# Second modulation, first half: weighted rows added up on VectorE and summed over partitions once, in place of matmuls per block

## The chip, the cores and the metric

One core of one Trainium2 chip. The metric is device microseconds for one execution of the whole program. The engines are called by their short names: PE (TensorE), DVE (VectorE), ACT (ScalarE), POOL (GpSimd), SP (SyncE, which issues the large loads).

## The reference, cut to what matters

The program is two transformer blocks one after the other. The change lies in the first one. A vector `c` of 1024 elements gives six rows of 1024 (shift, scale and gate, twice), which modulate the sequence (256 tokens, 1024 features) ahead of the token mixer and ahead of the mixture of experts:

```
sc = silu(c)
shift1, scale1, gate1, shift2, scale2, gate2 = split(sc @ w_mod + b_mod, 6)   # w_mod: 1024 x 6144
h = modulate(rms_norm(x, norm1_g), shift1, scale1)      # h * (1 + scale) + shift
y, yc = token_mixer(h, hc, P, last)                      # attention, GLA and Hyena branches
x = x + gate1 * y
h = modulate(rms_norm(x, norm2_g), shift2, scale2)
x = x + gate2 * grouped_moe(h, router_w, ...)            # 16 experts
```

"The second modulation" is the product for the last 4096 columns (gate1, shift2, scale2, gate2): `sc` (1024 long) times a 1024 x 4096 matrix, plus the bias `b_mod2`. Half 0 is its first 2048 columns. The token mixer projects `h` into columns for three branches, works them, weighs each by a gate, and merges:

```
m = sigmoid(g_hy) * (y_hy @ w_br_hy) + sigmoid(g_gla) * (y_gla @ w_br_gla) + sigmoid(g_att) * (y_att @ w_br_att)
y = m @ w_out
```

All data are float32. Most products are made as three F32R matmuls of high and low parts (`mm3`).

## The kernel before, in words

**Loads and splits.** SP loads weights as `raw` tiles of 128x2048 (1 MB) in an order that is fixed ahead (`take`, L552, gives them out; `load` issues the next ones when slots are free). Each matrix that goes through `mm3` is split into `w`: a high part by ACT and a low part by DVE, in pieces of 128x1024. The matrices of the second modulation are not split.

**The stage.** The loop over branches (L1414 on, inside `program`) runs attention, GLA, Hyena. In each it takes four blocks of gate columns (`w_brg`: 48 h matmuls of 128x256 each, rows `ps<-hH,w` and `ps<-hL,w`), in the attention branch six blocks of Hyena columns (`hyena_cols`, whose evacuations are the `uc` rows on ACT and DVE: one ACT activation, then two DVE operations on it, twice a block), in the GLA branch the `gate_cols`, and then the branch product (`w_br_att`: rows `ps<-ya,w`; `w_br_gla`: rows `ps<-yg,w`).

**Side jobs.** Attention, GLA and Hyena are generators beside these columns. `Side.tick` (L383 on) runs the next step of a job after a group of matmuls, when a model clock on PE, ACT and DVE (`Clocked`, L341) says that its inputs are there; so the order of the program is set when it is built, from the costs of the operations issued so far. An attention step for head h is `turn(h-2)` (transposes `ps<-c_base,e`, copied by ACT to `pT`), `scores(h)`, `weigh(h-3)` (rows `ps<-pT,kv`, split into `ya`), softmax and normalization.

**Second modulation.** Sixteen blocks of 128x2048, `mod_block(i)` (L1353), are put between the columns: blocks 0 to 3 behind the four `w_brg` blocks of attention, 4 to 7 behind the four `w_br_att` blocks, 8 to 15 in the other branches. For each, `mod_rows` (L815) issues four float32 matmuls (128x32 `cs` as the stationary operand, 512 columns each, the trace has two records for each) that go to four groups of 32 partitions of one PSUM bank, and over eight blocks add up to one half of the modulation. At the eighth the bias (`bm`) is added on DVE, and the generator `mod_spread` splits the 128x512 into `mrow`, spreads each 512 columns over all partitions by K=32 matmuls with `pick`, and copies them into `mod2` tiles. For half 0 it goes on: one of its tiles is transposed (`turned_half`, rows `ps<-c_base,mod`, copied to `h2T`), router logits are made of it (`ps<-par,h2T`), and DVE copies them to `shifted`. Each of blocks 8 to 15 first runs one step of that generator.

**End of the GLA branch.** DVE normalizes the GLA output into `oy`; PE transposes it (`ps<-c_base,oy`), ACT and DVE split that into `yg`, and `ps<-yg,w` follows. The Hyena job then transposes `uc` into `z`, multiplies by the transform (`z,fwd`) and goes on through `Y` (parts `YH`, `YL`).

Of the kernel before, what the change touches and what calls it, by code (L numbers as in the profile page):

```python
# [10 lines left out]
F32R = mybir.dt.float32r  # L11
I32 = mybir.dt.int32
AF = mybir.ActivationFunctionType
OP = mybir.AluOpType
# [4 lines left out]
D = 1024  # L19
# [363 lines left out]
class Side:  # L383
# [10 lines left out]
    def next(self):  # L394

        a = self.jobs[:2]
        return a[1] if len(a) > 1 and a[1][2] is a[0][0] and a[1][1] < a[0][1] else a[0]
# [22 lines left out]
def program(ctx, tc, A, out, dump=None):  # L420
# [5 lines left out]
    V, S, G, P = nc.vector, nc.scalar, nc.gpsimd, nc.tensor  # L426
    V, S, P = Clocked(V, "V"), Clocked(S, "S"), Clocked(P, "P")
# [4 lines left out]
    def T(shape, name, dt=F32, tag=None):  # L432
        n = 4
        for s in shape[1:]:
            n *= s
        if tag is None:
            for t, lim in (("us", 128), ("uh", 512), ("u1", 1024), ("u2", 2048), ("u4", 4096), ("u8", 8192)):
                if n <= lim:
                    tag = t
                    break  # L440
        uid[0] += 1
        t = sb.tile(list(shape), dt, tag=tag, bufs=BUFS.get(tag, 1), name=f"{name}{uid[0]}")
        return t

    def T2(shape, name):

        n = 4 * math.prod(shape[1:])
        if n > 4096:
            return T(shape, name + "H", F32R), T(shape, name + "L", F32R)
        t = T([shape[0], 2, *shape[1:]], name, F32R)  # L450
        return t[:, 0], t[:, 1]

    def PS(name="ps"):
        uid[0] += 1
        t = pp.tile([128, 512], F32, tag="ps", bufs=8, name=f"{name}{uid[0]}")
        return t
# [6 lines left out]
    def split(h, l, src):  # L463
        S.activation(h, src, AF.Copy)
        V.tensor_tensor(l, src, h, op=OP.subtract)
# [86 lines left out]
    def take(name, b, u=0):  # L552
        i, v = pieces[pos["take"]]
        assert order[i][:2] == (name, b) and u == v, (order[i], v, name, b, u)
        stream()
        pos["take"] += 1
        return halves.pop((i, u)) if order[i][4] is not None else raws.pop(i)
# [66 lines left out]
    def feat_block(name, b, x, per=1):  # L624

        for u in range(2):
            wh, wl = take(name, b, u)
            for j in range(per):
                g = u * per + j
                if g % 2 == 0:  # L630
                    ps = PS()
                lin_feat(wh, wl, j, x, ps[:, (g % 2) * 256:(g % 2) * 256 + 256])
                side.tick()
                if g % 2:
                    yield ps
# [10 lines left out]
    def C(name):  # L646
        g, sl = CCOLS[name]
        return cg[g][:, sl]
# [35 lines left out]
    pick = T([128, 128], "pick", F32R)  # L684
# [7 lines left out]
    st = {}  # L692
# [119 lines left out]
    cs = T([128, 8, 32], "cs", tag="cs")  # L812
    V.memset(cs, 0.0)

    def mod_rows(w, k, ps):  # L815
        for j in range(4):
            P.matmul(ps[32 * j:32 * j + 32], cs[:, k], w[:, 0, j * 512:j * 512 + 512], start=k == 0, stop=k == 7)
# [46 lines left out]
    mrow = T([128, 512], "mrow")  # L864
# [41 lines left out]
    def by_k(pair):  # L906
        return lambda k: (pair[0][:, k], pair[1][:, k])
# [164 lines left out]
    ps = PS()  # L1072
# [276 lines left out]


    acc2, mod2, spreads = {}, [], []

    def mod_block(i):  # L1353

        hf, k = divmod(i, 8)
        w = take("mod2", i)
        if hf:
            next(spreads[0], None)
        if k == 0:
            acc2[hf] = PS("mod")  # L1360
        mod_rows(w, k, acc2[hf])
        if k == 4:
            st["bm"] = bm = T([128, 512], "bm", tag="u4")
            V.memset(bm, 0.0)
            for j in range(4):
                S.dma_start(bm[32 * j:32 * j + 1], A["b_mod2"][:, hf * 2048 + j * 512:hf * 2048 + j * 512 + 512])
        if k == 7:
            bm = st["bm"]
            V.tensor_tensor(bm, acc2.pop(hf), bm, op=OP.add)
            spreads.append(mod_spread(st.pop("bm")))  # L1370
            if False:
                next(spreads[hf])

    rw = Pc("router_w").rearrange("p (k e) -> p k e", k=8)

    def turned_half(src, k4):
        pt = PS()
        for k in range(4):
            P.transpose(pt[:, k * 128:k * 128 + 128], src[:, (4 * k4 + k) * 128:(4 * k4 + k) * 128 + 128], ident)
        t = T([128, 512], "h2T")  # L1380
        S.activation(t, pt, AF.Copy)
        return t

    def logits(ts, ps, start, stop):

        for k in range(8):
            P.matmul(ps, ts[k // 4][:, k % 4 * 128:k % 4 * 128 + 128], rw[:, k], start=start and k == 0, stop=stop and k == 7)

    def mod_spread(rows):

        rH, rL = T2([128, 512], "mrow")
        split(rH, rL, rows)
        yield
        for a in range(2):
            t = T([128, D], "mod2")
            for n in range(2):
                ps = PS()
                q = slice(32 * (2 * a + n), 32 * (2 * a + n) + 32)
                P.matmul(ps, pick[q], rH[q], start=True, stop=False)
                P.matmul(ps, pick[q], rL[q], start=False, stop=True)  # L1400
                S.activation(t[:, n * 512:n * 512 + 512], ps, AF.Copy)
            mod2.append(t)
        yield
        if len(mod2) == 2:
            ts = [turned_half(mod2[1], k4) for k4 in range(2)]
            yield
            ps = PS()
            logits(ts, ps[:, :16], True, True)
            st["shifted"] = T([128, 16], "shifted", tag="uh")
            V.tensor_copy(st["shifted"], ps[:, :16])  # L1410

    msum = mH = mL = None
    n_mod = 0
    for b, br in ((2, "att"), (1, "gla"), (0, "hy")):  # L1414
        g = T([128, 8, 256], "gate")
        for j in range(4):
            ps, = feat_block("w_brg", 4 * b + j, by_k(hs[0]))
# [18 lines left out]
        for i in range(8 // per):  # L1436
            for j, ps in enumerate(feat_block("w_br_" + br, i, ys, per // 2)):
                c = slice(per * i + 2 * j, per * i + 2 * j + 2)
# [156 lines left out]
    def ahead(v, count):  # L1595
# [21 lines left out]
                           op0=OP.is_lt, op1=OP.mult)  # L1617
    low(0, 1)

    ps = PS()  # L1620
# [75 lines left out]
    with tc.If(full > CAP, label="full"):  # L1696
# [11 lines left out]
        for e in range(N_EXP):  # L1708
            def fetch(k, i, q):
                t = fw[turn[0] % 2]  # L1710
                turn[0] += 1
                b, c = i // 2, i % 2 * 2 + q
                if k == "down" and b % 2 and e > N_EXP - 3:
                    b, c = 2 * (N_EXP - 2 + q) + 1, e % 2 * 2 + i % 2
                nc.sync.dma_start(t, A["moe_" + k][b, :, c * 512:c * 512 + 512])
                return t

            for k in range(8):
                for q in range(2):
                    w = fetch("gu", 8 * e + k, q)  # L1720
                    for m in range(2):
                        P.matmul(gu[q, m], fT[m][:, k * 128:k * 128 + 128], w, start=k == 0, stop=k == 7)
            for m in range(2):
                hf, ht, ps = hfs[m], hts[m], gu[0, m]
# [6 lines left out]
            for k in range(4):  # L1731
                for n in range(2):
                    w = fetch("down", 4 * e + k, n)
# [89 lines left out]
    for w, n in (("a", 8), ("b", 16)):  # L1823
# [4 lines left out]
        k = T([128, 2 * n], "rk", tag="us")  # L1828
# [26 lines left out]
    for e in range(N_EXP):  # L1855
# [3 lines left out]
        ps = PS()  # L1859
# [504 lines left out]
```

## Time and profile before

| | |
|---|---|
| median of 3 runs | 1422.9 us (1419.89 to 1423.99) |
| profiled execution | 1417.77 us, span 1416.0 us |
| mean granted PE clock | 0.994 |
| PE busy | 1365.2 us, 96% of the span |
| DVE busy | 836.7 us, 59% |
| ACT busy | 635.8 us, 45% |

The span goes from the first to the last instruction of the profiled execution; its own time lies 1.8 us over the span. Nearly all operations are issued through one wrapper and carry its line, L379; so one reads the trace by the names of tiles. A row such as `mod<-raw,cs` gives the tile written and those read. Matmuls are pipelined and the ends in their rows are modelled, so for PE the distance from start to start is read, not the length of one record. Durations and stalls all come from this one execution.

### The profile page before, as it was taken

What the parts mean: (1) busy time and instruction counts of PE and PEld (TensorE: products, weight loads), DVE (VectorE), ACT (ScalarE), POOL (GpSimd) and SP (SyncE); (2) the same over time, 40 slices, a digit from 0 to 9 for tenths busy, and PEclk for the clock granted to TensorE, in tenths of its full rate; (3) what the DMA queues carried; (4) which work ended last, traced back from release to release, by engine and by line L of the source; (5) the groups of instructions that cost most, each with busy time, mean ns of one, the idle gap of its engine ahead of it and who ended that gap; (6) DMA issues with size and microseconds to landing.
All of it is one profiled execution on the core that took longest, in us unless ns stands there. A gap on an engine that the chain in (4) does not pass through costs nothing.

```text
span 1416.0 us, 20480 instructions
## 1 busy us (share of the span) xinstructions
PE 1365.2 (96%) x8334; PEld 1064.8 (75%) x8334; DVE 836.7 (59%) x1517; ACT 635.8 (45%) x1021; POOL 8.3 (1%) x15
## 2 busy tenths in 40 slices
PE   5999999999999899999999899999999998999998
PEld 2678899878797444343488679999978887999996
DVE  4777457445866511211475586666676888566675
ACT  4643465534433311111356555445536664455541
POOL 0000000000000000000000000000000000000000
PEclk9999999999999999999999999999999999999999
DMA  9523334635469799999742345655544354555630
GB/s 370 223 71 119 149 150 153 250 125 190 175 212 360 301 421 421 421 421 421 283 179 90 120 149 181 207 179 208 175 156 146 127 179 139 188 179 180 216 140 30
DMA packets 44482, 297.42 MB, mean 210 GB/s; under 512 B 5171, under 2 KB 6371, under 8 KB 10017
## 3 DMA queue, kind: packets, MB, share of 16 engines
q1 hardware_dynamic: 41868, 291.02, 54.6%
q10 hardware_dynamic: 1924, 3.27, 0.7%
q0 software_dynamic: 592, 1.79, 0.5%
q8 instruction: 67, 1.10, 0.3%
q14 instruction: 31, 0.25, 0.0%
HBM read 295.00 MB, written 1.05 MB: 209 GB/s over the span
## 4 chain that ended last, share of the span: by engine, by line
PE 58%; DVE 5%; ACT 2%; issue 1%; DVEq 0%; ACTq 0%
PE ps L379 48%; PE pd L379 7%; DVE w L379 1%; PE pa L379 1%; PE pq L379 1%; ACT pe L379 1%; DVE v L379 1%; PE oc L379 1%; DVE sm L379 1%; DVE rs L379 0%; ACT w L379 0%; DVE xL L379 0%; DVE rsa L379 0%; ACT xH L379 0%; ACT oc L379 0%
## 5 line engine op out<-in xcount | busy, mean ns | idle before, releaser
L379 DVE TENSOR_TENSOR w<-raw,w 128x1024 fp32r<-128x1024 f32 (+3 forms) x301 | 346.5, 1195 | 84.6 <-ACT w L379 83.5
L379 ACT ACTIVATE w<-raw 128x1024 fp32r<-128x1024 f32 (+3 forms) x301 | 293.5, 1033 | 10.8 <-DVE w L379 4.8
L379 PE MATMUL ps<-xH,w 128*128 128x256 f32 x1408 | 256.5, 283 | 0.6 <-ACT xH L379 0.6
L379 PEld LDWEIGHTS ps<-xH,w 128*128 128x128 f32 x1408 | 220.6, 192 | 1.8 <-ACT xH L379 1.1
L379 PE MATMUL ps<-xL,w 128*128 128x256 f32 x704 | 199.4, 283 | 0.7 <-DVE xL L379 0.7
L379 PE MATMUL ps<-w,xH 128*128 128x512 f32 (+2 forms) x544 | 150.3, 362 | 4.0 <-ACT xH L379 2.1
L379 PEld LDWEIGHTS ps<-xL,w 128*128 128x128 f32 x704 | 135.0, 192 | 1.8 <-DVE xL L379 1.1
L379 PE MATMUL pd<-w,fh 128*128 128x512 f32 x528 | 125.6, 395 | 0.0
L379 PE MATMUL ps<-raw,xg 128*64 128x512 f32 x512 | 120.0, 600 | 0.0
L379 PE MATMUL ps<-hH,w 128*128 128x256 f32 (+1 forms) x608 | 115.7, 287 | 0.0
L379 PEld LDWEIGHTS pd<-w,fh 128*128 128x128 f32 x528 | 98.2, 189 | 21.6
L379 PEld LDWEIGHTS ps<-w,xH 128*128 128x128 f32 x544 | 95.4, 189 | 19.3 <-ACT xH L379 4.0
L379 PEld LDWEIGHTS ps<-hH,w 128*128 128x128 f32 (+1 forms) x608 | 94.9, 187 | 7.9 <-issue 2.7
L379 PE MATMUL ps<-w,xL 128*128 128x512 f32 (+2 forms) x272 | 97.8, 360 | 1.9 <-DVE xL L379 1.7
L379 PE MATMUL ps<-w,hH 128*128 128x512 f32 (+1 forms) x288 | 88.1, 390 | 0.0
L379 PE MATMUL ps<-hL,w 128*128 128x256 f32 (+1 forms) x304 | 85.9, 283 | 0.0
L379 PEld LDWEIGHTS ps<-raw,xg 128*64 128x64 f32 x512 | 33.3, 137 | 55.7 <-issue 51.9
L379 DVE SCALAR_TENSOR_TENSOR fc<-ps,par,fc 128x255 f32<-128x255 f32 x88 | 42.4, 482 | 51.5 <-ACT fc L379 49.9
L379 ACT ACTIVATE fc<-ps,par 128x256 f32<-128x256 f32 x44 | 24.8, 564 | 92.3 <-PE ps L379 66.4
L379 PEld LDWEIGHTS ps<-w,hH 128*128 128x128 f32 x288 | 52.2, 188 | 13.8 <-issue 2.7
L379 PEld LDWEIGHTS ps<-w,xL 128*128 128x128 f32 x272 | 51.3, 189 | 11.9 <-DVE xL L379 5.1
L379 PE MATMUL ps<-raw,hid 128*64 128x512 f32 x256 | 57.4, 593 | 0.0
(445 smaller groups left out, 1858.7 us busy)
## 6 DMA issues: line engine op xcount, KB each, us to landing
raw<-in_moe_gu SPq DMA_DIRECT2D x63, 1024.0 KB, 14.1
raw<-in_moe_down SPq DMA_DIRECT2D x32, 1024.0 KB, 12.8
raw<-in_mod SPq DMA_DIRECT2D x24, 1024.0 KB, 5.0
raw<-in_ffn_gate SPq DMA_DIRECT2D x22, 1024.0 KB, 4.8
raw<-in_ffn_up SPq DMA_DIRECT2D x22, 1024.0 KB, 4.9
raw<-in_ffn_down SPq DMA_DIRECT2D x22, 1024.0 KB, 4.8
raw<-in_w_brg SPq DMA_DIRECT2D x12, 1024.0 KB, 5.9
raw<-in_ple_gate SPq DMA_DIRECT2D x8, 1024.0 KB, 4.8
```

The costliest lines, as they stand in the source:

```text
L379: return f(*args, **kw)
```

## The change

In half 0 (blocks 0 to 7) PE's matmuls go. A tile `acc` of 128x2048 is cleared on DVE at block 0, and its row 0 is loaded with the bias by a DMA on ACT's queue. In each of the eight blocks DVE adds the matrix, row by row times the block's column of `cs`, into `acc`, in two operations of 128x1024. At block 7 the new generator `mod_sums` takes the place of `mod_spread` for this half: for each 1024 columns it splits `acc` into `mrow` parts (ACT and DVE), and four F32R matmuls with a 128x128 matrix of ones sum over the partitions and spread the sum over all of them at once; ACT copies the results to `mod2`. Then come the transposes and the logits as before. The generator has five steps where `mod_spread` had four for this half, and blocks 8 to 15 still run one each. Half 1 stays as it was.

```diff
--- before.py
+++ after.py
@@ -1349,13 +1349,27 @@
 
 
     acc2, mod2, spreads = {}, [], []
+    ones = T([128, 128], "pick", F32R)
+    S.activation(ones, C("ones16"), AF.Copy, scale=16.0)
 
     def mod_block(i):
 
         hf, k = divmod(i, 8)
         w = take("mod2", i)
-        if hf:
-            next(spreads[0], None)
+        if not hf:
+
+            if k == 0:
+                st["acc"] = acc = T([128, 2048], "acc")
+                V.memset(acc, 0.0)
+                S.dma_start(acc[0:1], A["b_mod2"][:, :2048])
+            acc = st["acc"]
+            for n in range(2):
+                c = slice(n * 1024, n * 1024 + 1024)
+                V.scalar_tensor_tensor(acc[:, c], w[:, 0, c], cs[:, k, 0:1], acc[:, c], op0=OP.mult, op1=OP.add)
+            if k == 7:
+                spreads.append(mod_sums(st.pop("acc")))
+            return
+        next(spreads[0], None)
         if k == 0:
             acc2[hf] = PS("mod")
         mod_rows(w, k, acc2[hf])
@@ -1368,8 +1382,6 @@
             bm = st["bm"]
             V.tensor_tensor(bm, acc2.pop(hf), bm, op=OP.add)
             spreads.append(mod_spread(st.pop("bm")))
-            if False:
-                next(spreads[hf])
 
     rw = Pc("router_w").rearrange("p (k e) -> p k e", k=8)
 
@@ -1385,6 +1397,27 @@
 
         for k in range(8):
             P.matmul(ps, ts[k // 4][:, k % 4 * 128:k % 4 * 128 + 128], rw[:, k], start=start and k == 0, stop=stop and k == 7)
+
+    def mod_sums(acc):
+
+        for a in range(2):
+            rH, rL = T2([128, D], "mrow")
+            split(rH, rL, acc[:, a * D:a * D + D])
+            yield
+            t = T([128, D], "mod2")
+            for n in range(2):
+                ps = PS()
+                for r in (rH, rL):
+                    P.matmul(ps, ones, r[:, n * 512:n * 512 + 512], start=r is rH, stop=r is rL)
+                S.activation(t[:, n * 512:n * 512 + 512], ps, AF.Copy)
+            mod2.append(t)
+            yield
+        ts = [turned_half(mod2[1], k4) for k4 in range(2)]
+        yield
+        ps = PS()
+        logits(ts, ps[:, :16], True, True)
+        st["shifted"] = T([128, 16], "shifted", tag="uh")
+        V.tensor_copy(st["shifted"], ps[:, :16])
 
     def mod_spread(rows):
 
@@ -1401,14 +1434,6 @@
                 S.activation(t[:, n * 512:n * 512 + 512], ps, AF.Copy)
             mod2.append(t)
         yield
-        if len(mod2) == 2:
-            ts = [turned_half(mod2[1], k4) for k4 in range(2)]
-            yield
-            ps = PS()
-            logits(ts, ps[:, :16], True, True)
-            st["shifted"] = T([128, 16], "shifted", tag="uh")
-            V.tensor_copy(st["shifted"], ps[:, :16])
-
     msum = mH = mL = None
     n_mod = 0
     for b, br in ((2, "att"), (1, "gla"), (0, "hy")):
```

DVE, block 0 of the modulation in the attention branch, behind the low part of a gate column's weights. Before:

```order
228 L379 TENSOR_TENSOR w_1354<-raw_1262,w_1354 128x1024
229 L379 TENSOR_TENSOR ya_1417<-ps_1412,ya_1417 128x256
230 L379 TENSOR_REDUCE nb_1420<-ps_1404 128x1
231 L379 TENSOR_SCALAR nb_1420<-nb_1420,rs_640 128x1
232 L379 TENSOR_REDUCE nb_1423<-ps_1408 128x1
233 L379 TENSOR_SCALAR nb_1423<-nb_1423,rs_719 128x1
```

Now (`acc` is the new sum, `raw` the modulation matrix, `cs` the weights of its rows):

```order
228 L379 TENSOR_TENSOR w_1356<-raw_1264,w_1356 128x1024
229 L379 MEMSET acc_1361 128x2048
230 L379 SCALAR_TENSOR_TENSOR acc_1361<-raw_990,cs_105,acc_1361 128x1024 x2
231 L379 TENSOR_TENSOR w_1393<-raw_1366,w_1393 128x1024
232 L379 TENSOR_TENSOR ya_1446<-ps_1441,ya_1446 128x256
233 L379 TENSOR_REDUCE nb_1449<-ps_1433 128x1
234 L379 TENSOR_SCALAR nb_1449<-nb_1449,rs_640 128x1
```

The memset and the two additions of block 0 stand ahead of `ya` and the softmax rows behind it; so does the next low part `w`, which stood behind those rows before.

PE, the last attention steps, ahead of the branch product `ya,w` (`c_base,e`: the transposes of `turn`; `pT,kv`: `weigh`; `hH,w` and `hL,w`: Hyena columns). Before, first `turn(7)` and `weigh(6)`, and 34 rows later `weigh(7)`:

```order
697 L379 MATMUL ps_2063<-hH_315,w_1938 128x256
698 L379 MATMUL ps_2118<-c_base_80,e_1894 128x128 x4
699 L379 MATMUL ps_2124<-c_base_80,e_1897 128x128 x4
700 L379 MATMUL ps_2130<-pT_2001,kv_592 128x256 x4
701 L379 MATMUL ps_2147<-hH_315,w_1973 128x256
702 L379 MATMUL ps_2147<-hL_316,w_1973 128x256
```

```order
733 L379 MATMUL ps_2147<-hL_316,w_2025 128x256
734 L379 MATMUL ps_2147<-hH_315,w_2025 128x256
735 L379 MATMUL ps_2207<-pT_2117,kv_592 128x256 x4
736 L379 MATMUL ps_2214<-ya_1417,w_2060 128x256 x6
737 L379 MATMUL ps_2214<-ya_1634,w_2060 128x256 x6
```

Now:

```order
726 L379 MATMUL ps_2098<-hL_316,w_1952 128x256
727 L379 MATMUL ps_2098<-hH_315,w_1952 128x256
728 L379 MATMUL ps_2183<-c_base_80,e_2016 128x128 x4
729 L379 MATMUL ps_2189<-c_base_80,e_2019 128x128 x4
730 L379 MATMUL ps_2195<-pT_2123,kv_592 128x256 x4
731 L379 MATMUL ps_2203<-pT_2182,kv_592 128x256 x4
732 L379 MATMUL ps_2210<-ya_1446,w_2032 128x256 x6
```

`turn(7)`, `weigh(6)` and `weigh(7)` follow one another behind the last Hyena column, with the branch product right behind.

PE, end of the GLA branch (`oy`: transposes of the normalized output; `mrow,pick` in the second listing: the matmuls with ones for the second 1024 columns). Before:

```order
1037 L379 MATMUL ps_3088<-hH_315,w_2962 128x256
1038 L379 MATMUL ps_3140<-c_base_80,oy_3012 128x128 x2
1039 L379 MATMUL ps_3140<-c_base_80,oy_3032 128x128 x2
1040 L379 MATMUL ps_3147<-c_base_80,oy_3012 128x128 x2
1041 L379 MATMUL ps_3147<-c_base_80,oy_3032 128x128 x2
1042 L379 MATMUL ps_3160<-par_63,h2T_3073 128x16 x4
1043 L379 MATMUL ps_3160<-par_63,h2T_3080 128x16 x4
1044 L379 MATMUL mod_2657<-raw_2931,cs_105 32x512 x4
1045 L379 MATMUL ps_3182<-yg_2994,w_3035 128x256 x24
```

Now:

```order
1025 L379 MATMUL ps_3049<-hH_315,w_2934 128x256
1026 L379 MATMUL ps_3101<-c_base_80,oy_2984 128x128 x2
1027 L379 MATMUL ps_3101<-c_base_80,oy_3004 128x128 x2
1028 L379 MATMUL ps_3108<-c_base_80,oy_2984 128x128 x2
1029 L379 MATMUL ps_3108<-c_base_80,oy_3004 128x128 x2
1030 L379 MATMUL ps_3122<-mrow_3040,pick_1258 128x512 x2
1031 L379 MATMUL ps_3126<-mrow_3040,pick_1258 128x512 x2
1032 L379 MATMUL mod_2584<-raw_2837,cs_105 32x512 x4
1033 L379 MATMUL ps_3141<-yg_2966,w_3007 128x256 x24
1034 L379 MATMUL ps_3171<-yg_2966,w_3035 128x256 x24
1035 L379 MATMUL ps_3203<-c_base_80,mod_3121 128x128 x4
1036 L379 MATMUL ps_3210<-c_base_80,mod_3121 128x128 x4
```

The matmuls with ones stand where the router logits (`par,h2T`) stood; the transposes of `mod`, before 34 rows ahead of `oy`, come two product groups behind it, and the logits have left the listing for a place after the first Hyena transform.

DVE at the same place. Before:

```order
388 L379 TENSOR_TENSOR oy_3032<-o_2584,rs_3020 128x512
389 L379 TENSOR_TENSOR oy_3032<-oy_3032,gog_2844 128x512
390 L379 TENSOR_TENSOR w_3035<-raw_2965,w_3035 128x1024
391 L379 TENSOR_TENSOR w_3063<-raw_2965,w_3063 128x1024
392 L379 TENSOR_TENSOR w_3113<-raw_3086,w_3113 128x1024
393 L379 TENSOR_TENSOR yg_2994<-ps_3140,yg_2994 128x512
394 L379 TENSOR_TENSOR yg_2994<-ps_3147,yg_2994 128x512
```

Now:

```order
395 L379 TENSOR_TENSOR oy_3004<-o_2660,rs_2992 128x512
396 L379 TENSOR_TENSOR oy_3004<-oy_3004,gog_2716 128x512
397 L379 TENSOR_TENSOR w_3007<-raw_2937,w_3007 128x1024
398 L379 TENSOR_TENSOR w_3035<-raw_2937,w_3035 128x1024
399 L379 TENSOR_TENSOR mrow_3040<-acc_1361,mrow_3040 128x1024
400 L379 TENSOR_TENSOR w_3074<-raw_3047,w_3074 128x1024
401 L379 TENSOR_TENSOR yg_2966<-ps_3101,yg_2966 128x512
402 L379 TENSOR_TENSOR yg_2966<-ps_3108,yg_2966 128x512
```

A split of `acc` into `mrow` has come between the second and the third low part `w`, ahead of the evacuations `yg`.

## Rows read from the trace of the kernel before

**Rows 1.** Page, part 1: busy time, share of the span and instructions of each engine.
```profile
PE 1365.2 (96%) x8334; PEld 1064.8 (75%) x8334; DVE 836.7 (59%) x1517; ACT 635.8 (45%) x1021; POOL 8.3 (1%) x15
```

**Rows 2.** Windows, 170 to 290 us: stretch and length, busy us (instructions) per engine, clock, DMA.
```profile
170.00:180.00 10.00, 10.00 (x73) 8.60 (x72) 5.58 (x11) 4.93 (x9) 0.00 (x0) 1.00 0.44 178
...
sum 120.00, PE 120.00 PEld 106.64 DVE 68.88 ACT 69.77 POOL 0.00; mean PE 10.00 PEld 8.89 DVE 5.74 ACT 5.81 POOL 0.00
```

**Rows 3.** Groups by form on PE, 160 to 290 us: count, busy us, mean ns, idle.
```profile
L379 PE MATMUL mod<-raw,cs 128*32 128x512 f32 x64 | 8.5, 605 | 0.0
```

**Rows 4.** Tile `mod`: count, duration ns min/median/max, first and last start, form.
```profile
L379 PE MATMUL mod<-raw,cs x192: 592/593/1062, 13.8 to 400.3; 128*32 128x512 f32 x192
...
L379 DVE SCALAR_TENSOR_TENSOR mod<-mod,g2n x1: 1225/1225/1225, 446.1 to 446.1; 128x1024 f32<-128x1024 f32 x1
```

**Rows 5.** Timeline of PE around one block: start, us, engine, operation, count [idle before].
```profile
186.58 1.07 PE L379 MATMUL mod<-raw,cs 128*32 128x512 f32 x8
187.58 0.39 PE L379 MATMUL ps<-hH,w 128*128 128x256 f32 x1
```

**Rows 6.** Timeline of DVE, a memset in the GLA branch.
```profile
282.84 0.91 DVE L379 MEMSET att<- 128x1024 f32 x1 [0.16 <-issue]
```

**Rows 7.** Timeline of DVE, start of two attention steps.
```profile
173.31 0.42 DVE L379 TENSOR_TENSOR ya<-ps,ya 128x256 fp32r<-128x256 f32 x1 [5.64 <-ACT ya L379]
...
184.24 0.42 DVE L379 TENSOR_TENSOR ya<-ps,ya 128x256 fp32r<-128x256 f32 x1 [4.21 <-ACT ya L379]
```

**Rows 8.** Page, part 6: DMA issues, KB each, median us to landing.
```profile
raw<-in_mod SPq DMA_DIRECT2D x24, 1024.0 KB, 5.0
```

**Rows 9.** Timeline of SP's queue, the load of block 2.
```profile
158.67 0.33 SPq L515 DMA_DIRECT2D raw<-in_mod  x1
```

**Rows 10.** Timeline of PE, spreading half 0 and the block behind it.
```profile
314.21 0.74 PE L379 MATMUL ps<-mrow,pick 32*128 32x512 f32 x6
...
315.96 1.07 PE L379 MATMUL mod<-raw,cs 128*32 128x512 f32 x8
```

**Rows 11.** Timeline of PE, 128x512 F32R matmuls of the `gate` columns.
```profile
329.84 0.63 PE L379 MATMUL ps<-w,hH 128*128 128x512 f32 x2
...
330.53 0.62 PE L379 MATMUL ps<-w,hH 128*128 128x512 f32 x2
```

**Rows 12.** Timeline of ACT, end of the hyena columns.
```profile
238.60 1.08 ACT L379 ACTIVATE pT<-ps 128x512 f32<-128x512 f32 x2 [1.43 <-PE ps L379]
...
246.51 0.56 ACT L379 ACTIVATE uc<-ps,par 128x256 f32<-128x256 f32 x1 [1.38 <-PE ps L379]
248.15 0.56 ACT L379 ACTIVATE uc<-ps,par 128x256 f32<-128x256 f32 x1 [1.07 <-DVE uc L379]
```

**Rows 13.** Timeline of PE, end of attention.
```profile
237.96 1.04 PE L379 MATMUL ps<-c_base,e 128*128 128x128 f32 x8
...
246.31 1.89 PE L379 MATMUL ps<-pT,kv 128*128 128x256 f32 x8
247.85 1.43 PE L379 MATMUL ps<-ya,w 128*128 128x256 f32 x9
```

**Rows 14.** Timeline of DVE, end of the GLA branch.
```profile
349.86 3.49 DVE L379 TENSOR_TENSOR w<-raw,w 128x1024 fp32r<-128x1024 f32 x3
353.26 1.28 DVE L379 TENSOR_TENSOR yg<-ps,yg 128x512 fp32r<-128x512 f32 x2
```

**Rows 15.** Timeline of PE, end of the GLA branch.
```profile
341.72 1.04 PE L379 MATMUL ps<-c_base,mod 128*128 128x128 f32 x8
...
350.70 1.86 PE L379 MATMUL ps<-par,h2T 128*128 128x16 f32 x16
```

**Rows 16.** Waits of PE, 330 to 420 us: total us, times, longest.
```profile
PE ps L379 <- ACT z L379: 1.1, 1, 1.1
PE ps L379 <- DVE z L379: 1.1, 1, 1.1
PE ps L379 <- DVE YL L379: 0.8, 1, 0.8
```

## The prediction

> **What bounds the kernel now.** I read the page's busy line first: PE is busy 96% of the span, DVE 59%, ACT 45% [rows 1]. That is an average, so next I read busy time by stretch, where the change works: from 170 to 290 us PE is busy 120.00 us of 120, DVE 68.88, which leaves DVE 51 us idle [rows 2]. There no engine but PE sets the pace: a PE microsecond taken out should shorten the program, a DVE microsecond put in costs nothing while nobody waits for it. The granted clock is 1.00 there, the 2.4 GHz level, so no change of clock enters the sum.
>
> **What is removed.** 64 records of `mod<-raw,cs` stand between 160 and 290 us; together they cover 8.5 us of PE [rows 3]. One record takes 593 ns [rows 4], but the eight of a block run side by side: they start at 186.58, and the next h matmul starts at 187.58 [rows 5], 1.00 us a block and 8.0 for eight by that distance, 8.5 by the grouped row. I take the grouped row, as it holds all eight blocks: **-8.5 us**. Summing single records would give 64 x 0.593 = 38 us; the window shows that they overlap. In the Trainium skill, "TensorE: Matmul & The Clock Gate", section "Measured speedup vs the span model", three column tiles are given 2.38 times the speed of matmuls one behind the other. By that figure alone a block would be an estimated 8 x 0.593 / 2.38 = 2.0 us and the saving 16; the trace shows 1.00 to 1.07, so the measurement decides.
>
> **What is added on DVE.** Sixteen 128x1024 operations of two tensors and a scalar. The trace has that kind once, 1225 ns [rows 4]: 19.6 us. A memset of 128x1024 takes 0.91 [rows 6], so about 1.8 for 128x2048. Two 128x1024 `mrow` splits come in place of one of 128x512, and the `bm` add goes. That is some 23 us into 51 us of idle. The idle lies in pieces: DVE idles 5.64 us before the attention step at 173.31 and 4.21 before the one at 184.24 [rows 7]. A block's 2.45 us fits in either. The tight place is block 0: memset 1.8, then the `b_mod2` row by a DMA on ACT's queue, on which the accumulations wait, then 2.45. The DMA is between nothing and the 5.0 us that a whole megabyte of `in_mod` takes [rows 8]; even at 5.0 the sum, 9.3 us, overruns 5.64 by 3.6, and the next gap of 4.21 absorbs it. Priced at 0. Behind a waiting accumulation stand the low parts of `w` and `ya`, which PE needs; if that cover is gone each block costs up to its 2.45 (rival B). ACT's second `w` split of the block stands behind the DMA issue, with the same reserve.
>
> `acc` also holds one slot of the size that SP's loads use, from block 0 to the second split, so an SP load can have to wait for one more release. Block 2's matrix is issued at 158.67 [rows 9] and read at 186.58 [rows 5], 28 us ahead with 5.0 to land. Priced at 0. The order on SP and POOL does not change.
>
> **Spreading the sums.** Before, eight K=32 matmuls spread half 0: from 314.21 to the next block at 315.96, 1.75 us [rows 10]. After, eight 128x512 F32R matmuls by `ones`; three of that size take 0.69 us (329.84 to 330.53) [rows 11], so 8 x 0.23 = 1.8, entered at two places rather than one: **+0.3**, ends 0 and 0.5.
>
> **The end of attention.** The side jobs are placed by a model clock, in which PE has become cheaper and DVE dearer, so they come later in PE's row. `weigh(7)` stood 34 rows behind `turn(7)`; now `turn(7)`, `weigh(6)` and `weigh(7)` follow one another. `weigh(7)` needs both copies of `pT`, which stand on ACT behind two `uc` activations with DVE's `uc` work between: from the first `uc` at 246.51 to the end of the second, 248.71, then the two copies, 1.08: 3.28 us [rows 12], and the first starts 0.20 after PE's group is through (246.31, where `weigh` follows it). PE has `turn(7)` to do, 1.04, and `weigh(6)`, 1.54 (246.31 to 247.85) [rows 13]. The wait is 0.20 + 3.28 - 1.04 - 1.54 = **+0.9**. Ends: 0, if ACT comes to `uc` earlier against PE; 2.1, if DVE has a `w` split of 1.2 (a third of the 3.49 of [rows 14]) ahead of `uc`.
>
> **The end of the GLA branch.** The second pair of `ones` matmuls stands right behind the `oy` transposes and needs `mrow`'s low part. DVE makes that behind the `oy` chain and two `w` splits: three splits run from 349.86 for 3.49 [rows 14], so the third in line, now `mrow`'s, is done at 353.35. PE has the transposes behind it at 350.70 [rows 15], its high-part matmul at about 351. Wait: 353.35 - 351 = **+2.4**, the row's own order; ends 0 (the splits run earlier, their inputs being there) and 2.6. Before, 1.86 us of router matmuls stood at that place and hid DVE's queue [rows 15]. The `yg` evacuations move one split later, about 1.2 us, which this wait and the `mod` block behind it cover. The transposes of `mod`, 1.04 us [rows 15], also leave the rows ahead of `oy`, where they covered the `oy` chain; some GLA state matmuls come in their place: **+0.3**, ends 0 and 1.0.
>
> **Given back.** Those 1.04 us now stand between `yg` groups ahead of the hyena transform, where PE waited 1.1 for ACT's `z` and 1.1 for DVE's; the router matmuls stand ahead of a 0.8 wait for `YL` [rows 16]. Work that fills a wait is free there: 1.0 + 0.8 = **-1.8**, ends 0 and -3.0, all three waits. The GLA loops move some ten rows later among the `gate` columns: 0, ends -1 and +1.
>
> **Sum.** -8.5 + 0.3 + 0.9 + 2.4 + 0.3 - 1.8 = **-6.4 us**. The profiled execution (1417.77) would go to 1411.4. It lies 5.1 under the median of the runs, 1422.9, so the forecast of the median is 1422.9 - 6.4 = **1416.5**. A difference of 0.3% (4.3 us) is about what a measurement of this kernel can tell from none.
>
> **Rivals.**
> *A. The stalls take most of it.* If the three waits reach their upper ends (2.1, 2.6, 1.0), spreading costs 0.5, the loops 1, and nothing is given back, the sum is -8.5 + 7.2 = -1.3: 1421.6. For it: short PE work leaves exactly the places where it covered DVE. Against: PE waits only 3.0 us between 330 and 420 now [rows 16].
> *B. DVE's queue holds PE, slower.* If DVE works strictly in order, an accumulation that waits for its matrix or for the `b_mod2` row holds `ya`, `w` and the softmax steps behind it. If PE waits for each block in full it is 8 x 2.45 - 8.5 = +11: 1434. It decides once the additions in one attention step exceed that step's idle (4.2 to 5.6 us), or a load comes later than its 28 us lead. For it: `yg`, whose transposes PE had behind it at 350.70, starts on DVE only at 353.26, when the splits ahead of it end [rows 14, 15]. Against: 2.45 is half of a step's idle. The Trainium skill has the rule in "Perfetto Trace Analysis", section "Tensor Engine Instruction (MATMUL, LD_WEIGHTS)": ScalarE and VectorE are strict FIFOs, while PE can pull weight loads ahead. It speaks against putting DVE work in front of what PE needs; by that rule, the trace agrees.
> *C. No new wait.* With the three waits at nothing and the rest as taken it is -8.5 + 0.3 - 1.8 = -10.0: 1412.9. For it: the waits rest on two places in the order, and DVE and ACT have idle time ahead of both. Against: PE arrives at both with less work of its own.
>
> **How the numbers follow.** Forecast case 0.55, A 0.23, B 0.13, C 0.09. The forecast case reaches past 1418.6, the bound of "same", with about 0.06 of its chance. Faster 0.49 + 0.09 = 0.58; same 0.06 + 0.23 = 0.29; slower 0.13. The range goes from 1411.5 (C, less some of the spread of runs, which lie 4.1 apart) to 1424.0 (A with that spread and the mild end of B); most of B is left out.
>
> **What will show it.** Right: no `mod<-raw,cs` on PE from 160 to 290 us, and PE still full there; the accumulations near 1.23 us each; PE's last `ya,w` matmul some 7 us earlier; a wait of about 1 for ACT's `pT` ahead of the first; one of 2 to 2.5 for DVE's `mrow` behind `oy`; the `z` waits 1 shorter and `YL` near nothing; from 390 us on the same distances, moved. Wrong: PE waits for `w` or `ya` inside the attention steps (B), the waits from 240 to 390 sum to over 6 (A), or a changed wait in the expert stage, which this sum takes to follow PE.

## The result and the profile after

The kernel after takes 1414.89 us in the median of 7 runs (1411.61 to 1416.93), the kernel before 1422.9 (1419.89 to 1429.15, 7 runs beside them): ratio 0.9936, 95% interval 0.9913 to 0.9960. It is faster by 8.0 us of medians, 0.4 to 0.9% by the interval; 1416.5 had been forecast.

The page of the profiled execution (1416.68 us), against [rows 1]: PE has lost 64 records and little busy time, DVE has gained 22 us.

```profile
PE 1362.9 (96%) x8270; PEld 1066.4 (75%) x8270; DVE 858.6 (61%) x1533; ACT 637.8 (45%) x1023; POOL 8.3 (1%) x15
```

The two profiled executions can't be subtracted as they are, 1416.68 against 1417.77. Long ahead of the changed stretch, in the first weight products, the granted clock stood at 0.53 for a while in the one after. Windows of before, then of after (length, busy us and instructions per engine, clock, DMA share, GB/s):

```profile
30.00:40.00 10.00, 9.46 (x52) 2.96 (x50) 9.51 (x10) 4.33 (x4) 0.23 (x1) 1.00 1.01 416
```

```profile
30.00:40.00 10.00, 10.00 (x28) 2.96 (x31) 6.37 (x8) 3.82 (x2) 0.17 (x1) 0.53 1.02 424
```

The first transpose of an attention step starts at 159.51 before and at 164.44 after, 4.93 us later, with the same instructions ahead of it and one more, the copy on ACT that makes the matrix of ones (at 157.75). That copy is not the reason: e1, e6 and e7 below have it too, and start at 159.46 to 159.69. So from here on **distances from that transpose** are read: to the first `ya,w` matmul, to the first `yg,w`, and to the `mask` matmul ahead of the experts (470.66 before, 469.15 after). To `mask` it is 311.15 before and 304.71 after: **-6.44 us**. From `mask` to the end of the span it is 945.34 and 945.75, so the expert stage only moved.

The stretch of the change, to be held against [rows 2], whose PE sum was 120.00 and DVE sum 68.88:

```profile
170.00:180.00 10.00, 10.00 (x74) 9.53 (x74) 7.74 (x7) 3.76 (x6) 0.00 (x0) 1.00 0.64 215
...
240.00:250.00 10.00, 8.83 (x56) 7.80 (x55) 7.08 (x14) 5.99 (x11) 0.00 (x0) 1.00 0.27 102
...
sum 120.00, PE 118.83 PEld 111.33 DVE 91.27 ACT 72.82 POOL 0.00; mean PE 9.90 PEld 9.28 DVE 7.61 ACT 6.07 POOL 0.00
```

PE is still full but for one hole near 248; DVE has taken 22.4 us more without PE waiting for an addition. The tile `acc` (count, ns min/median/max, first and last start):

```profile
L379 DVE SCALAR_TENSOR_TENSOR acc<-raw,cs,acc x16: 1276/1278/1283, 176.4 to 285.3; 128x1024 f32<-128x1024 f32 x16
L379 ACT ACTIVATE mrow<-acc x2: 1047/1052/1057, 291.2 to 339.1; 128x1024 fp32r<-128x1024 f32 x2
L379 DVE TENSOR_TENSOR mrow<-acc,mrow x2: 1219/1222/1226, 292.3 to 347.1; 128x1024 fp32r<-128x1024 f32 x2
L379 DVE MEMSET acc<- x1: 1765/1765/1765, 173.0 to 173.0; 128x2048 f32 x1
```

The waits of PE from 240 to 480 us (total, times, longest), to be held against [rows 16]:

```profile
PE ps L379 <- DVE mask L379: 4.4, 1, 4.4
PE ps L379 <- DVE mrow L379: 2.3, 1, 2.3
PE ps L379 <- ACT pT L379: 1.2, 1, 1.2
PE ps L379 <- DVE z L379: 1.1, 1, 1.1
...
PE ps L379 <- DVE S L379: 0.3, 1, 0.3
PE ps L379 <- ACT z L379: 0.2, 1, 0.2
```

Both forecast waits are there, 2.3 for `mrow` (2.4 forecast) and 1.2 for `pT` (0.9 forecast). The wait for ACT's `z` has gone from 1.1 to 0.2, the one for `YL`, 0.8, is gone, DVE's `z` is unchanged; before's waits of 0.5 for `att` and 0.4 for `ke` are also gone, which the sum did not have (the row for `ke` stands further down):

```profile
PE ps L379 <- DVE att L379: 0.5, 1, 0.5
```

`mask`, 4.4, was there before. The `mrow` wait in the timelines of PE and of DVE:

```profile
344.45 1.39 PE L379 MATMUL ps<-c_base,oy 128*128 128x128 f32 x8
345.60 0.47 PE L379 MATMUL ps<-mrow,pick 128*128 128x512 f32 x1
348.37 0.96 PE L379 MATMUL ps<-mrow,pick 128*128 128x512 f32 x3 [2.30 <-DVE mrow L379]
349.26 1.33 PE L379 MATMUL mod<-raw,cs 128*32 128x512 f32 x8
350.53 7.24 PE L379 MATMUL ps<-yg,w 128*128 128x256 f32 x48
```

```profile
344.83 2.35 DVE L379 TENSOR_TENSOR w<-raw,w 128x1024 fp32r<-128x1024 f32 x2
347.10 1.22 DVE L379 TENSOR_TENSOR mrow<-acc,mrow 128x1024 fp32r<-128x1024 f32 x1
348.24 1.22 DVE L379 TENSOR_TENSOR w<-raw,w 128x1024 fp32r<-128x1024 f32 x1
349.37 1.28 DVE L379 TENSOR_TENSOR yg<-ps,yg 128x512 fp32r<-128x512 f32 x2
```

DVE runs two `w` splits whose readers, the `yg,w` matmuls, come later on PE, then the split that PE stands waiting for. The 48 `yg,w` matmuls behind take 7.24 where they take 6.02 in e6 below: from 350 to 355 the granted clock is 0.67.

### The profile page after: what moved, and what is told of

Same layout as the page of the kernel before. It is cut to its first block, busy times and chain, and to the rows that moved or that the text cites. A ratio compares the mean times of both kernels' runs of the same rounds, so it can differ in the third digit from the quotient of the medians.

```text
span 1414.9 us, 20369 instructions
## 1 busy us (share of the span) xinstructions
PE 1362.9 (96%) x8270; PEld 1066.4 (75%) x8270; DVE 858.6 (61%) x1533; ACT 637.8 (45%) x1023; POOL 8.3 (1%) x15
## 4 chain that ended last, share of the span: by engine, by line
PE 58%; DVE 5%; ACT 2%; issue 1%; DVEq 0%; ACTq 0%
PE ps L379 48%; PE pd L379 7%; DVE w L379 1%; PE pa L379 1%; PE pq L379 1%; ACT pe L379 1%; DVE v L379 1%; PE oc L379 1%; DVE sm L379 1%; DVE rs L379 0%; ACT w L379 0%; DVE xL L379 0%; DVE rsa L379 0%; ACT xH L379 0%; ACT oc L379 0%
```

## The experiments

All times are distances from the first attention transpose in a profiled execution, in us; "clock falls" counts the stretches between 160 and 445 us in whose 10 us windows the granted clock stood under 0.99 (neighbouring windows as one). The ratio is that of all runs to the runs of the kernel before.

| kernel | to `ya,w` | to `yg,w` | to `mask` | clock falls | median us | ratio (95%) |
|---|---|---|---|---|---|---|
| before | 88.34 | 193.98 | 311.15 | 0 | 1422.9 | 1 |
| after | 85.19 | 186.09 | 304.71 | 1 | 1414.89 | 0.9936 (0.9913 to 0.9960) |
| e1 second split early | 85.18 | 183.83 | 302.41 | 0 | 1413.04 | 0.9927 (0.9903 to 0.9952) |
| e2 old order | 83.62 | 191.99 | 310.13 | 2 | 1420.05 | 0.9975 (0.9955 to 0.9995) |
| e3 both | 83.62 | 187.72 | 309.52 | 2 | 1418.50 | 0.9958 (0.9935 to 0.9982) |
| e4 matmuls back on PE | 89.93 | 194.97 | 312.38 | 0 | 1421.42 | 0.9986 (0.9970 to 1.0002) |
| e6 no additions | 85.19 | 185.83 | 303.25 | 0 | 1412.15 | 0.9934 (0.9913 to 0.9956) |
| e7 old order for attention alone, early split | 83.62 | 182.40 | 300.96 | 0 | 1407.65 | 0.9903 (0.9873 to 0.9933) |
| e8 second half on DVE too | 85.18 | 200.42 | 334.80 | 4 | 1443.63 | 1.0144 (1.0117 to 1.0171) |
| e9 additions twice | 98.35 | 201.34 | 319.39 | 3 | 1428.29 | 1.0039 (1.0019 to 1.0059) |

**What the removed matmuls were worth, and what the additions cost: e4 and e6.** In e4 the 32 matmuls are issued again at their old places and everything else keeps its order:

```diff
+            if k == 0:
+                acc2[0] = PS("mod")
+            for j in range(4):
+                nc.tensor.matmul(acc2[0][32 * j:32 * j + 32], cs[:, k], w[:, 0, j * 512:j * 512 + 512], start=k == 0, stop=k == 7)
             if k == 7:
+                acc2.pop(0)
                 spreads.append(mod_sums(st.pop("acc")))
             return
```

> The kernel after with the 32 removed matmuls put back on PE (their result unused), at the old places, the order of everything else unchanged; DVE does its additions as well. Theory (the gain is PE's 8.5 us and nothing else, and the DVE part is free): 304.7 + 8.5 = 313.2 from the first attention transpose to the `mask` matmul; the waits for `pT` and `mrow` unchanged. Rival (part of the gain came from elsewhere, or PE time there is partly covered): clearly under 313.

In e6 the additions are left out, and the model clock is still charged for them. Half 0 is then the bias alone, so only the stretch up to `mask` is compared:

```diff
-                V.scalar_tensor_tensor(acc[:, c], w[:, 0, c], cs[:, k, 0:1], acc[:, c], op0=OP.mult, op1=OP.add)
+                Clocked(Nothing(), "V").scalar_tensor_tensor(acc[:, c], w[:, 0, c], cs[:, k, 0:1], acc[:, c], op0=OP.mult, op1=OP.add)
```

> The kernel after without its sixteen additions on DVE (the sum is left out: half 0 of the second modulation is the bias alone), the order of everything else unchanged. Theory (the additions cost nothing): the waits for `pT` (1.2) and `mrow` (2.3) are the same and the distance from the first attention transpose to the `mask` matmul is 304.7 with the clock low behind the second wait, 303.5 with it high. Rival (the additions are paid somewhere): shorter than 303 with the clock high, and the `mrow` wait smaller.

e4 came to 312.38, e6 to 303.25; both have the waits of the kernel after. The waits of e6 from 160 to 445:

```profile
PE ps L379 <- DVE mrow L379: 2.3, 1, 2.3
PE ps L379 <- ACT pT L379: 1.2, 1, 1.2
```

The kernel after is 1.46 longer than e6. Of that 1.21 lies between `yg,w` and the Hyena transform (14.14 against 12.93) and the rest in the `mod` block ahead of it (1.27 from start to start, elsewhere 1.00): just the stretch in which the clock of the kernel after was low. Up to `ya,w` the two agree to 0.01. So twenty microseconds of additions on DVE cost PE nothing that can be seen: theory holds. e4 against e6, neither with a fall of the clock, gives the eight blocks as 9.13 on PE. A block between two h matmuls costs 1.08 there too (164.06, 164.27, 165.26: 1.20 less the usual 0.12):

```profile
164.06 0.28 PE L379 MATMUL ps<-hH,w 128*128 128x256 f32 x1
164.27 1.07 PE L1372 MATMUL mod<-raw,cs 128*32 128x512 f32 x8
165.26 0.38 PE L379 MATMUL ps<-hH,w 128*128 128x256 f32 x1
```

In the new order one of the eight stands behind a `weigh`: that `weigh` starts at 173.39 and has its block 1.82 behind it, where `ya,w` followed in 1.54 [rows 13]. Added up from start to start between the first attention transpose and `mask`, less the waits, the eight blocks themselves are 7.96 of the 9.13; the rest is in longer distances of rows around them (h matmuls 0.58, `ya,w` 0.32, `weigh` 0.28).

**The `mrow` wait: e1.** The second split is issued one step earlier, ahead of the GLA branch's last chain; PE's order is the same:

```diff
         for a in range(2):
-            rH, rL = T2([128, D], "mrow")
-            split(rH, rL, acc[:, a * D:a * D + D])
-            yield
+            if a == 0:
+                rH, rL = T2([128, D], "mrow")
+                split(rH, rL, acc[:, :D])
+                yield
+                sH, sL = T2([128, D], "mrow")
+                split(sH, sL, acc[:, D:])
+            else:
+                yield
+                rH, rL = sH, sL
```

> Measured from the first attention transpose to the `mask` matmul ahead of the experts (311.15 us in the profile before, 304.71 in the one after). Theory (the wait of 2.3 us for `mrow` arises only from the place of the second split on DVE's row): the `mrow` wait is gone, but the third `w` split and `yg` move up by one split only, so PE, with less to do ahead of `yg`, waits there for DVE's `yg` about 1.2; net -1.1, 303.6. If the clock fell behind that wait (granted 0.83 from 350 to 360), it is 1.00 there now and another 1.2 comes back: 302.4. Rival 1: the wait is simply paid at `yg`, 2.3 there, 304.7 as before. Rival 2: nothing takes its place, 302.4 with the clock still low, 301.2 without.

302.41, the value of the theory with the clock up; the second rival's 302.4 was for a low clock and no new wait, and neither is the case. The `mrow` wait is gone and shorter ones have taken its place:

```profile
PE ps L379 <- DVE yg L379: 0.9, 1, 0.9
PE ps L379 <- ACT qkT L379: 0.5, 1, 0.5
```

Against e6, whose clock stayed up with the wait in place, the edit is worth only 0.84: 2.3 less 0.9 for `yg` and 0.5 for `qkT`, ahead of which ACT now makes the split's high part. In whole runs the edit is inside the noise.

**The order of the side jobs: e2, e3, e7.** In e2 the model clock is charged for the matmuls that are no longer there and not for the additions; so attention and GLA stand on PE as in the kernel before:

```diff
-                V.memset(acc, 0.0)
+                nc.vector.memset(acc, 0.0)
...
+            Clocked.now["P"] += 4 * 512 / 2400 * 4
+            if k in (4, 7):
+                Clocked.now["V"] += 0.07 + 512 / 960
             for n in range(2):
                 c = slice(n * 1024, n * 1024 + 1024)
-                V.scalar_tensor_tensor(acc[:, c], w[:, 0, c], cs[:, k, 0:1], acc[:, c], op0=OP.mult, op1=OP.add)
+                nc.vector.scalar_tensor_tensor(acc[:, c], w[:, 0, c], cs[:, k, 0:1], acc[:, c], op0=OP.mult, op1=OP.add)
```

> The side jobs stand in the order of the kernel before, the work is that of the kernel after. Theory (the wait for `pT` comes from the later order of attention alone): no wait for `pT` ahead of the last `weigh`, -1.2; the 0.5 wait for `att` in the GLA loop returns; the `mrow` wait of 2.3 stays. From the first attention transpose to the `mask` matmul 304.7 - 1.2 + 0.5 = 304.0. Rival: the additions on DVE delay an attention step in this order too, so that a wait of about 1.2 for DVE's `ya` or ACT's `pT` shows elsewhere: 305.

The `pT` wait went, and `ya,w` starts 1.57 earlier. But `mask` is at 310.13, 5 to 6 beyond both the theory and the rival: with the same work, the old order gives back nearly all that the change gains. The waits, 160 to 445:

```profile
PE ps L379 <- DVE mrow L379: 4.3, 1, 4.3
...
PE ps L379 <- DVE att L379: 1.0, 1, 1.0
PE ps L379 <- DVE acc L1371: 1.0, 1, 1.0
```

and the clock behind the first of them (windows), low again from 350 to 360 behind the 4.3:

```profile
260.00:270.00 10.00, 10.00 (x58) 8.62 (x59) 6.32 (x7) 7.33 (x10) 0.00 (x0) 0.83 0.54 203
```

```profile
350.00:360.00 10.00, 8.52 (x43) 5.61 (x44) 4.74 (x5) 5.18 (x6) 0.00 (x0) 0.68 0.69 263
```

So the loss has two parts. Against e6, e2 is 6.88 longer up to `mask`. The waits are 2.9 of it; the other 4.0 lies in longer distances between starts, most of it in the rows behind the two falls of the clock (`ya,w` alone 1.8). The whole runs fit this: eleven of e2's twelve had a mean clock of 0.982 to 0.989, and the one at 0.993 took 1413.83, some 2 us over the 1411.61 and 1411.84 of the kernel after at 0.994.

The wait put down to `acc` stands ahead of `ps<-wa,gin` at 257.98. Its input `wa` comes by small DMAs, issued from 250.82 on, which land 5.3 us after their issue. In the kernel before the matmul started 7.29 us behind the first of these issues (250.64, 257.93) without a wait, a modulation block of 1.07 ahead of it; here the block is gone, PE comes that much sooner, and 0.97 of it is a wait. By the same 5.3 the last of them, issued at 251.66, lands near 256.96, and the matmul starts 1.0 behind that (in e3 1.2). That these DMAs are what PE waits for, and not the addition that the trace names, is read from such times and was not tried.

e3 takes both edits.

> Both edits. Theory (the waits are independent and add up): 304.7 - 1.1 - 0.7 = 302.9 from the first attention transpose to the `mask` matmul, 301.7 if the clock stays up; 2 to 3 us faster than the kernel after, ratio to the kernel before about 0.9935 - 0.0018. Rival: what one edit gains the other gives back (the GLA chain comes at another time against DVE's splits), no better than the better of the two.

309.52, worse than either theory or the early split alone: the second outcome named there. The wait moved to `yg` in full:

```profile
PE ps L379 <- DVE yg L379: 2.7, 1, 2.7
PE ps L379 <- DVE acc L1371: 1.2, 1, 1.2
```

e7 separates the two parts of the order: the clock is charged for blocks 0 to 3 alone, so attention stands early and GLA late, with the early split.

```diff
+            if k < 4:
+                Clocked.now["P"] += 4 * 512 / 2400 * 4
             for n in range(2):
                 c = slice(n * 1024, n * 1024 + 1024)
-                V.scalar_tensor_tensor(acc[:, c], w[:, 0, c], cs[:, k, 0:1], acc[:, c], op0=OP.mult, op1=OP.add)
+                (nc.vector if k < 4 else V).scalar_tensor_tensor(acc[:, c], w[:, 0, c], cs[:, k, 0:1], acc[:, c], op0=OP.mult, op1=OP.add)
```

> The kernel with the early second split, and the model clock is charged for the first four removed blocks as before, so that the attention steps stand as in the kernel before while the GLA steps stand as in the kernel after. Theory (the late GLA order is worth having, the late attention order costs the `pT` wait): no `pT` wait, no wait for `wa`, 302.4 - 1.6 = 300.8 from the first attention transpose to the `mask` matmul, ratio to before about 0.9915. Rival (the waits of the old order come from the old place of attention, not of GLA): 303 or more.

300.96 against 300.8 expected, the shortest of all, and the fastest runs: 1407.65 in the median, ratio 0.9903. Its interval still touches that of the kernel after; the trace is 3.75 shorter up to `mask`, with these waits left (160 to 445):

```profile
PE ps L379 <- DVE z L379: 1.1, 1, 1.1
PE ps L379 <- DVE yg L379: 0.9, 1, 0.9
PE ps L379 <- ACT qkT L379: 0.5, 1, 0.5
```

So the late attention order cost its 1.57: e7 starts `ya,w` by that much earlier than the kernel after. And the late GLA order was worth having: e3 and e7 differ only in what the model clock is charged for blocks 4 to 7, and e3 is 8.56 longer, 4.0 by waits and 4.5 by longer distances between starts, with two falls of the clock where e7 has none.

**How much more DVE could take: e5, e9, e8.** e5 does every addition a second time.

```diff
+            for n in range(2):
+                c = slice(n * 1024, n * 1024 + 1024)
+                nc.vector.scalar_tensor_tensor(acc[:, c], w[:, 0, c], cs[:, k, 1:2], acc[:, c], op0=OP.mult, op1=OP.add)
```

> The kernel after, with every addition on DVE done twice (the second with weight 0, so the sum stays), 19.6 us more on DVE, nothing moved on PE. In the profile after DVE is busy 33.2 of 40 us from 170 to 210 us and 27.5 of 40 from 250 to 290. Theory (DVE's additions are free only up to its idle time in each stretch): the first four blocks' 9.8 us overrun the first stretch by 3, the second stretch holds them; 304.7 + 3 = 308 from the first attention transpose to the `mask` matmul, with PE waiting for DVE's `w` or `ya` in the attention steps, 2 to 7 with the clock. Rival 1 (DVE's reserve is larger than its busy share says): 304.7. Rival 2 (each addition holds PE in full): 324.

The weight was not 0: that column of `cs` belongs to the context, so the sum changed, the tokens took another path through the experts (2466 us in all), and only the stretch up to `mask` can be read: 313.01. e9 repeats it with a tile of zeros in place of `cs[:, k, 1:2]`.

> The doubling of the additions again, with a weight that is 0 in fact (the other column that the earlier one took holds the weights of the context's modulation). DVE's work up to the experts is the same as there, so the stretch from the first attention transpose to the `mask` matmul should repeat: 313.0, or about 311.5 if the clock falls less often, with waits near 2 ahead of two attention transposes and one ahead of the GLA products; all executions together about 7 to 9 us slower than the kernel after. Rival (that stretch was disturbed by chance): near 304.7.

319.39 and 1428.29 us, 14.7 longer than the kernel after up to `mask` and slower than the kernel before (ratio 1.0039). The theory's 308 was too low both times, and the repeat was not a repeat: for the same additions, PE's waits for `sm`, `kw` and `w` sum to 5.6 in e5 and to 9.4 in e9, and the clock fell further in e9 (0.92, 0.74, 0.98 and 0.68 in its windows from 190 to 260, against 0.83 twice in e5). Why the waits differ is open. Against e6, e9 is 16.1 longer up to `mask`: 8.2 by waits and 8.0 by longer distances between starts, with its three falls of the clock; e5 is 9.8 longer, 4.4 and 5.4. PE now waits on the attention chain (e9, 160 to 445):

```profile
PE ps L379 <- DVE sm L379: 7.9, 3, 4.7
PE ps L379 <- DVE mrow L379: 2.3, 1, 2.3
...
PE ps L379 <- DVE kw L379: 1.0, 1, 1.0
```

and DVE shows how (timeline of e9): 2.48 of additions, 2.48 again, and only then `ya` and the normalization, whose first half ends at 199.18; the transposes of it start at 199.32 on PE, 2.86 late.

```profile
191.69 2.48 DVE L379 SCALAR_TENSOR_TENSOR acc<-raw,cs,acc 128x1024 f32<-128x1024 f32 x2
194.08 2.48 DVE L1374 SCALAR_TENSOR_TENSOR acc<-raw,zero,acc 128x1024 f32<-128x1024 f32 x2
196.47 0.42 DVE L379 TENSOR_TENSOR ya<-ps,ya 128x256 fp32r<-128x256 f32 x1
...
198.69 0.49 DVE L379 TENSOR_SCALAR e<-e,sm 128x512 f32<-128x512 f32 x1
```

e8 takes the change further instead: half 1 is summed on DVE as well, with the early split.

```diff
-        mod_rows(w, k, acc2[hf])
...
+        acc = st["acc"]
+        for n in range(2):
+            c = slice(n * 1024, n * 1024 + 1024)
+            V.scalar_tensor_tensor(acc[:, c], w[:, 0, c], cs[:, k, 0:1], acc[:, c], op0=OP.mult, op1=OP.add)
+        if k == 7:
+            spreads.append((mod_sums2 if hf else mod_sums)(st.pop("acc")))
```

> The kernel with the early second split, and the second half (blocks 8 to 15) on DVE in the same way; its PE matmuls go as well. In the profile after, DVE is busy 73.9 of 110 us from 290 to 400, and the change adds 23. Theory (a block is worth 1.07 on PE wherever PE is the pace, but in the Hyena part the end of a DVE chain sets it): -8.5 of PE and +4 of longer waits for `z`, `yg` and `YL`: 298 from the first attention transpose to the `mask` matmul. Rival 1: no more waits, 294. Rival 2: DVE's row holds PE by 2.45 for each of the six blocks in the GLA and Hyena products, over 302.4 (the early split alone).

334.80, 32.4 longer than e1, far over the 302.4 beyond which the second rival put it: the runs are 1.4% slower than before. Its waits sum to 25.4 more than e1's, and its distances between starts are 7.0 longer although the 8.0 of matmuls are gone, with four falls of the clock. The three largest waits, 160 to 445:

```profile
PE ps L379 <- DVE oy L379: 8.8, 2, 5.2
PE ps L379 <- ACT YH L379: 5.8, 2, 3.2
PE ps L379 <- ACT qkT L379: 4.8, 1, 4.8
```

They are not waits for `acc` but for the GLA and Hyena chains, which are late: the model clock has moved these side jobs once more, and additions stand among them on DVE. Which of the two weighs more was not tried. DVE is not full: from 290 to 400 us it is busy 73.84 of 110, as in the kernel after (73.90).

## Why the prediction was right, point by point

The forecast was -6.4 us; the distance to `mask` fell by 6.44, the medians fell by 8.0, with an interval that holds both. The profiled execution did not go to 1411.4, since it has the low clock of its first 50 us, 4.9; two of the seven runs, at a mean clock of 0.994 like the profile before, took 1411.61 and 1411.84.

That the sum hit the trace so closely is partly luck. With the clock up (e6), the change is worth 311.15 - 303.25 = 7.90, so the mechanism gained 1.5 more than forecast, and the fall of the clock behind the `mrow` wait, of which the sum had nothing, took 1.46 back in this execution. Single terms were off in both directions as well. One by one:

- **The removed matmuls, -8.5.** 9.13 by e4 against e6, in the new order; 8.6 by the 1.08 of a block between h matmuls.
- **The additions at 0.** Right, by e6. The kind takes 1.28 us rather than 1.225; the memset 1.765 (1.8 forecast); DVE stood 1.7 us waiting for the `b_mod2` row, and its idle time absorbed it all.
- **The `pT` wait, +0.9.** 1.17, of that mechanism: gone in e2 and e7. Between the two `uc` of ACT lay 1.70 rather than 1.07, because a `w` split stood on DVE ahead of them, as the upper end had it.
- **The `mrow` wait, +2.4.** 2.30, for the reason given: gone in e1.
- **Given back, -1.8.** 0.9 at ACT's `z` and 0.8 at `YL`: 1.65.
- **Spreading, +0.3.** It is +0.8, the term furthest off for its size. The four matmuls at the first place take 1.21 from their start to that of the next kind, the four at the second 1.36 without their wait, 2.57 in all against 1.75 before; the sum had 8 x 0.23 and only 0.2 for the second place. And of the 1.75, 0.36 was no work but a wait (`ke`) that the reading of [rows 10] missed. The first place after, and the row of before with the wait:

```profile
298.84 1.28 PE L379 MATMUL ps<-mrow,pick 128*128 128x512 f32 x4
300.05 1.07 PE L379 MATMUL mod<-raw,cs 128*32 128x512 f32 x8
```

```profile
315.30 0.73 PE L379 MATMUL ps<-mrow,pick 32*128 32x512 f32 x2 [0.36 <-ACT ke L379]
```

- **`oy`, +0.3, and the GLA loops, 0.** No wait for `oy` came. In the GLA steps the wait of 0.5 for `att` went and one of 0.3 for `S` came.
- **What no term had.** With these sizes the terms add up to -6.7, against -7.90 in the trace. The other 1.2 is in distances between starts that the sum took as unchanged; `gv,ke` (0.75) and `yg,w` (0.55) shortened most.

Of the signs named, the waits from 240 to 390 sum to 5.1, short of the 6 for A. PE's last `ya,w` matmul came some 11 us earlier rather than 7, because the first GLA steps, 4.3 us on PE, stood ahead of the last `ya,w` group before and stand behind it now.

What the sum did not see at all is what e2, e3 and e7 show: the moved order was not only the source of two waits, its GLA part was needed. In the old order the same work ends at 310.13, 1.0 under before. There PE, with less of its own work, comes to the GLA steps before their inputs, and loses about as much by the low clock behind these waits as by the waits themselves.

Of the rivals, A (the stalls take most) did not come, but e2 comes to its size, by waits at other places and by the clock. B, DVE's row holding PE, is real at twice the additions: e9 is its mechanism, in `ya` and the normalization, and slower than before. It named the point at which it decides, the idle time of an attention step (4.2 to 5.6); 2.48 us fitted, 4.96 did not. C (no new wait, -10.0) was not met. e7 comes to its size, -10.2, but with new waits of 0.9 and 0.5, and by moving two things.

## What to carry to other kernels

Work can be taken from the engine that sets the pace and given to one with idle time, if the piece fits into the idle time *of each step* on that engine's row: here 2.5 us per step cost nothing, and 5 us cost 15 in all (e9), about half of it as waits and half behind a lowered clock. The busy share alone does not tell: the same exchange taken one stage further, with DVE no more than two thirds busy, lost 32 us, though the order of the chains moved there too. And where the order comes from a model clock, removing work moves everything else; look at where each short step lands and what it waits for, and try the charges separately: charging blocks 4 to 7 in the old way or the new was worth 8.6 us (e3 against e7), more than the change itself.

## What the runs showed that was not expected

A wait on PE can cost more than itself. Behind the 2.30 us `mrow` wait the granted clock went to 0.67 from 350 to 355 us, towards the lower of its two levels (1.2 of 2.4 GHz), and 1.46 us were lost; behind the same 2.3 wait it fell in e5 and e9 too (0.69 from 355 to 360, 0.78 from 360 to 365), and in e4 and e6 it stayed at 1.00. The windows of the kernel after and of e6 around it:

```profile
345.00:350.00 5.00, 2.70 (x18) 1.40 (x18) 5.00 (x6) 3.60 (x6) 0.00 (x0) 0.99 0.86 305
350.00:355.00 5.00, 5.00 (x31) 4.47 (x28) 1.79 (x4) 4.74 (x4) 0.00 (x0) 0.67 1.02 410
```

```profile
340.00:345.00 5.00, 2.56 (x19) 1.44 (x18) 5.00 (x6) 3.38 (x6) 0.00 (x0) 1.00 0.81 293
345.00:350.00 5.00, 5.00 (x45) 4.51 (x38) 3.24 (x5) 4.73 (x5) 0.00 (x0) 1.00 1.00 379
```

PE was busy for about half of the five microseconds ahead in both. The longer waits of e3 (2.7), e2 (4.3) and e9 (4.7) were each followed by a fall, and so were those of 1.0 and 1.2 ahead of `wa,gin` in e2 and e3, but not the one of 1.2 for `pT` in five executions. In e2, e3, e5 and e9 the longer distances between starts, most of them where the clock was low, make up about half of the loss. What decides stays open; runs of one kernel differ by some microseconds with their mean clock (1411.61 at 0.994, 1416.41 at 0.987 in the kernel after), and that is a reason to compare distances within the trace and to look at the clock beside them.
